# A hybrid decoder layer on one core: the work on the memory tiles tied behind the weight splits of the output products, and six of eight squares of x emitted behind the next weights

## The chip, the cores and the metric

The kernel runs on one core of one Trainium2 chip. The metric is the device time of one execution in microseconds (us). The engines are PE (TensorE, the matrix multiplier, with its weight loads PEld), ACT (ScalarE), DVE (VectorE), POOL (GpSimd) and SP (SyncE, which here only issues DMAs). Each engine works through its own list of instructions in order, and waits where an instruction's semaphore has not come yet.

## The reference

A decoder layer on 512 tokens of width 1024, all in float32: a SwiGLU feed-forward block, a mixer with a state-space group and a differential-attention group side by side, a cross-attention into a fixed memory of 256 tokens, a second SwiGLU block and a final norm.

```
x = x + 0.5 * swiglu(rms_norm(x, norm_ffn1_w[l]), ffn1_w_in[l], ffn1_w_out[l])
x = x + hybrid_mixer(rms_norm(x, norm_mix_w[l]), w_in_mix[l], ...)
x = x + memory_cross_attention(rms_norm(x, norm_cross_w[l]),
                               rms_norm(mem, norm_mem_w[l]),
                               w_cq[l], w_ck[l], w_cv[l], w_co[l])
x = x + 0.5 * swiglu(rms_norm(x, norm_ffn2_w[l]), ffn2_w_in[l], ffn2_w_out[l])
return rms_norm(x, norm_final_w)
```

Two pieces of it matter here. `rms_norm(mem, norm_mem_w)` needs the sum of squares of the memory and the memory times its gain, and both depend on inputs alone, so they can be computed early. `rms_norm(x, norm_mix_w)` needs the sum of squares of x after the first feed-forward block.

## The kernel before, in words

**Products.** A float32 product is done as three products of reduced operands: every operand is split into a high part (`wh`, written by an ACT copy, line 155) and a low part (`wl`, the rest, written by a DVE subtraction, line 156), and PE adds high by high, high by low and low by high. So each weight tile of 128 x 1024 or 128 x 512 that a DMA brings (`wr`, six buffers) costs one ACT and one DVE instruction before PE can use it, and the high and low tiles have three buffers each.

**The first feed-forward block** is done in three thirds of its hidden width. Each third first makes hidden tiles (`ffn_quads`, products `qa`, `qe`, `qb`) and then multiplies them by the output weights (`out_blocks`, products `oa`, `oe`, `ob`). Both use a block scheme with seven products of sums in place of eight: `block_tiles` makes from a hidden tile the operands `g11`, `s31`, `s24` and `g` (a few DVE subtractions and four splits). In the last tile of a third these are made at once, between the last hidden product and the output products. `out_blocks` then runs seven products, in the program's names: `oa` with block 11 and `oe` with the operand S1 interleaved, `ob` with S2, `oa` with block 12, `ob` with S3, `oe` with S4, `ob` with block 22. Each product has its weights in two parts in the last third: one of 128 x 1024 (twelve matmuls of 512 columns) and one of 128 x 512 (six). After a product, `update` adds its result to a tile of x on DVE, and on the last third calls `each`, which is `square`: an ACT square of that x tile with a running sum (`junk`, `squares`), for the mixer's norm.

**Work beside it.** When the last third reaches its output products, two generators are spawned. `prepare` builds a table of position biases, which ends with a DMA from DRAM to DRAM of 2.6 MB on ACT's queue (`rel_z`, line 609). `memory_in` loads the memory (four DMAs) and then, for each of eight memory tiles, emits under `behind(recent)` a square (ACT, `nacc` for the first tile and `nsq` for the others), the addition of the square to a sum (DVE, `nacc`) and a split of the tile times its gain (`hm`, ACT line 159 and DVE line 160). After the feed-forward block PE transposes x back (`pxf`) and multiplies the memory keys (`pck`, eight products, each with a weight tile `in_wck`).

**What sets the order.** `Order` runs the generator of matmuls and the spawned ones by a hand-kept clock. That is the order in which instructions are recorded; a scheduler may then put the instructions of ACT, DVE and PE in another order, while SP and POOL keep the recorded one. `behind(ins)` ties what is recorded in its block behind the instructions `ins` on the same engine. `recent` is a list that holds the two split instructions of the newest weights from `load_w`; the weights of `out_blocks` come from its own function `weights`, which leaves `recent` as it is.

Of the kernel before, what the change touches and what calls it, by code (L numbers as in the profile page):

```python
# [100 lines left out]
def body(tc, a, dbg=None):  # L101
# [13 lines left out]
    def nm(s):  # L115
        uid[0] += 1
        return f"{s}_{uid[0]}"

    def s2(s, dt=F32, shape=(P, T)):
        if math.prod(shape[1:]) <= T // 2:  # L120
            return sp.tile(list(shape), dt, tag="s1", name=nm(s), bufs=NHALF)
        return sp.tile(list(shape), dt, tag="s2", name=nm(s))
# [17 lines left out]
    last, start, last_sum, recent, newest, newest_mm = [], [], [], [], [], []  # L140
    V, S, G = nc.vector, nc.scalar, nc.gpsimd
    od = Order()
# [9 lines left out]
    def split_into(hi, lo, src, scale=None):  # L152
        if scale is None:
            return (
                S.activation(hi, src, AF.Copy),  # L155
                V.tensor_tensor(lo, src, hi.bitcast(F32), ALU.subtract),  # L156
            )
        return (
            S.activation(hi, src, AF.Copy, scale=scale),
            V.scalar_tensor_tensor(lo, src, scale, hi.bitcast(F32), ALU.mult, ALU.subtract),  # L160
        )
# [388 lines left out]
    squares = small("squares", 8, bufs=1)  # L550

    def square(tb, n):
        junk = s2("junk")
        S.activation(junk, x[4 * n + tb], AF.Square, accum_out=squares[:, 4 * n + tb : 4 * n + tb + 1])

    def fin1():
        od.spawn(normed(st_mix, C_MIX, h, squares), 2.0)
        od.spawn(block_sums_in_dram(), 10.0)

    od.spawn(st1.finish(), 18.0)  # L560
    od.add(ffn1(h1, wa_s, beside, square, fin1))


# [641 lines left out]
    def out_blocks(blocks, sums, g, col4, ncol4, each=None, finale=None, clean=True):  # L1205


        n = len(g)
        parts = [(k, min(k + 2, n)) for k in range(0, n, 2)]

        def fetch(of, part):
            raw = wp.tile([P, (part[1] - part[0]) * T], F32, tag="wr", name=nm("wr"), bufs=6)
            nc.sync.dma_start(raw, of[:, part[0] * T : part[1] * T])
            return raw

        def weights(of, part, raw=None):
            if raw is None:
                raw = of(part) if callable(of) else fetch(of, part)
            w = raw.shape[1]
            hi = wp.tile([P, w], R32, tag="wh", name=nm("wh"))  # L1220
            lo = wp.tile([P, w], R32, tag="wl", name=nm("wl"))
            split_into(hi, lo, raw)
            return hi, lo

        def some(ps, w, which, part, t, first):
# [9 lines left out]
        def product(ps, of, which, first=False):  # L1235
            for part in parts:
                w = weights(of, part)
                for t in range(2):
                    yield from some(ps[t], w, which, part, t, first)
# [74 lines left out]
        with tc.manual_schedule(engines={mybir.EngineType.DVE, mybir.EngineType.Activation}):  # L1314
            yield from at_last(parts, blocks, sums, e_ps, b_ps, fetch, weights, some, update, finale)
# [156 lines left out]
```

## Time and profile before

| | |
|---|---|
| median of 3 runs | 1328.78 us (1328.25 to 1331.37) |
| the profiled execution, its time | 1328.03 us |
| its span, first to last instruction | 1326.2 us |
| mean granted clock of PE | 0.992 |
| busy in the span: PE, DVE, ACT, POOL | 98%, 75%, 53%, 10% |

Times in the trace count from the span's start. A row of a timeline gives the start, the duration, the engine, the line, the operation, output <- input, and in brackets how long the engine sat idle before it and what ended that wait. Rows that follow one another and are alike are merged, with their count and total. The granted clock is 1.00 when PE gets its full clock. Matmuls overlap: the distance between two starts is what one costs, not its own duration.

The output products of the last third of the first feed-forward block begin at 312.65 us in this trace, and the memory keys at 362.47 us.

### The profile page before, as it was taken

To read this page: it belongs to the slowest core of one execution; us is meant where nothing else is said; L and a number is where in the kernel's file an instruction comes from. 1 tells how busy PE (TensorE), PEld (TensorE's weight loads), DVE (VectorE), ACT (ScalarE), POOL (GpSimd) and SP (SyncE) were. 2 spreads that over 40 slices of the span, in tenths; PEclk is the share of its full clock that TensorE was granted. 3 is DMA by queue.
4 is the path that set the end of the run, shared out by engine and by line. 5 is a ranking of instruction groups with operands and counts; after the bars stand their busy time and mean duration, and the time that the engine had idled before them with its cause. 6 is when DMAs were issued, how large, how long until landed. Compare 5 with 4: busy or idle time off the path is not lost.

```text
span 1326.2 us, 20148 instructions
## 1 busy us (share of the span) xinstructions
PE 1296.8 (98%) x7728; PEld 1128.5 (85%) x7728; DVE 988.7 (75%) x1570; ACT 708.6 (53%) x1192; POOL 127.5 (10%) x143
## 2 busy tenths in 40 slices
PE   9999999997999999999999999999999999999996
PEld 7898998896797778777788877888889999989995
DVE  6988789787786586557867787645678878877886
ACT  6544556455654475346644556434465645555564
POOL 0001000000030011010112121120001000000001
PEclk9999999998999999999999999999999999999998
DMA  7557767874794523763465547784238876666662
GB/s 272 159 172 212 178 174 204 216 202 112 238 325 152 170 64 96 250 179 96 96 190 183 166 136 222 206 203 147 65 96 242 227 234 176 190 194 178 187 204 86
DMA packets 69432, 235.29 MB, mean 177 GB/s; under 512 B 8072, under 2 KB 9576, under 8 KB 68984
## 3 DMA queue, kind: packets, MB, share of 16 engines
q1 hardware_dynamic: 52912, 180.19, 40.4%
q0 software_dynamic: 12880, 44.62, 18.9%
q10 hardware_dynamic: 3544, 9.20, 2.0%
q8 instruction: 61, 1.00, 0.3%
q14 instruction: 35, 0.29, 0.1%
HBM read 231.82 MB, written 50.91 MB: 213 GB/s over the span
## 4 chain that ended last, share of the span: by engine, by line
PE 88%; issue 6%; DVE 3%; ACT 1%; POOL 1%; DMA 0%; POOLq 0%; SPq 0%; ACTq 0%; DVEq 0%
PE qb L240 12%; PE pm L146 9%; PE qe L240 8%; PE qa L240 8%; PE ob L1232 6%; PE pxbc L146 5%; PE oe L1232 4%; PE oa L1232 4%; PE pk L146 3%; PE pq L146 3%; PE pcq L146 3%; PE pv L146 3%; PE pz L146 2%; PE pck L146 2%; PE pa L146 2%
## 5 line engine op out<-in xcount | busy, mean ns | idle before, releaser
L155 ACT ACTIVATE wh<-wr 128x1024 fp32r<-128x1024 f32 (+1 forms) x329 | 334.7, 1020 | 367.5 <-issue 55.8
L156 DVE TENSOR_TENSOR wl<-wr,wh 128x1024 fp32r<-128x1024 f32 (+1 forms) x329 | 386.0, 1176 | 143.0 <-ACT wh L155 138.1
L146 PE MATMUL pxbc<-hnh,wh 128*128 128x512 f32 x128 | 52.3, 408 | 0.0
L146 PE MATMUL pxbc<-hnh,wl 128*128 128x512 f32 x128 | 50.3, 393 | 0.0
L146 PE MATMUL pxbc<-hnl,wh 128*128 128x512 f32 x128 | 50.2, 392 | 0.0
L741 ACT ACTIVATE ec<-ec,mn 128x512 f32<-128x512 f32 (+3 forms) x64 | 35.4, 555 | 24.1 <-DVE mn L740 24.0
L240 PE MATMUL qe<-s31h,wl 128*128 128x256 f32 x152 | 43.1, 283 | 0.0
L240 PE MATMUL qa<-h11h,wh 128*128 128x256 f32 x152 | 43.1, 283 | 0.0
L240 PE MATMUL qa<-hmh,wh 128*128 128x256 f32 x152 | 43.0, 283 | 0.0
L240 PE MATMUL qa<-hml,wh 128*128 128x256 f32 x152 | 43.0, 283 | 0.0
L240 PE MATMUL qa<-hmh,wl 128*128 128x256 f32 x152 | 43.0, 283 | 0.0
L240 PE MATMUL qb<-s31l,wh 128*128 128x256 f32 x152 | 43.0, 283 | 0.0
L240 PE MATMUL qb<-s31h,wl 128*128 128x256 f32 x152 | 43.0, 283 | 0.0
L240 PE MATMUL qe<-s24h,wh 128*128 128x256 f32 x152 | 43.0, 283 | 0.0
L240 PE MATMUL qe<-s24l,wh 128*128 128x256 f32 x152 | 43.0, 283 | 0.0
L240 PE MATMUL qe<-s24h,wl 128*128 128x256 f32 x152 | 43.0, 283 | 0.0
L240 PE MATMUL qb<-hmh,wh 128*128 128x256 f32 x152 | 43.0, 283 | 0.0
L240 PE MATMUL qb<-hml,wh 128*128 128x256 f32 x152 | 43.0, 283 | 0.0
L240 PE MATMUL qb<-hmh,wl 128*128 128x256 f32 x152 | 43.0, 283 | 0.0
L240 PE MATMUL qa<-h11h,wl 128*128 128x256 f32 x152 | 43.0, 283 | 0.0
L240 PE MATMUL qb<-s31h,wh 128*128 128x256 f32 x152 | 43.0, 283 | 0.0
L240 PE MATMUL qa<-h11l,wh 128*128 128x256 f32 x152 | 43.0, 283 | 0.0
(447 smaller groups left out, 4188.6 us busy)
## 6 DMA issues: line engine op xcount, KB each, us to landing
wr<-in_f2q SPq DMA_DIRECT2D x44, 512.0 KB, 4.3
wr<-in_f1q SPq DMA_DIRECT2D x40, 512.0 KB, 4.5
wr<-in_f1b SPq DMA_DIRECT2D x30, 512.0 KB, 4.6
isum<-in_f2q SPq DMA_DIRECT2D x22, 512.0 KB, 6.0
wr<-isum SPq DMA_DIRECT2D x22, 512.0 KB, 6.4
wsum<-in_f2b SPq DMA_DIRECT2D x20, 512.0 KB, 5.9
wr<-wsum SPq DMA_DIRECT2D x20, 512.0 KB, 4.6
wr<-in_f1q POOLq DMA_DIRECT2D x16, 512.0 KB, 7.0
```

The costliest lines, as they stand in the source:

```text
L146: newest_mm[:] = [nc.tensor.matmul(out, w, x, start=start, stop=stop).ins]
L155: S.activation(hi, src, AF.Copy),
L156: V.tensor_tensor(lo, src, hi.bitcast(F32), ALU.subtract),
L240: newest_mm[:] = [nc.tensor.matmul(out, a_[:, wc], b_, start=first and f == 0 and kp == 0 and j == 0, stop=kp == n - 1 and j == 2, skip_gr ...
L741: S.activation(ec[:, :n], ec[:, :n], AF.Exp, bias=mn, scale=-1.0, accum_out=sm[c][:, i : i + 1])
L1232: newest_mm[:] = [nc.tensor.matmul(ps, a_[:, ts], b_[:, ws], start=first and k == 0 and j == 0, stop=k == n - 1 and j == 2, skip_group_che ...
```

## The change

```diff
@@ square
     def square(tb, n):
+        if n == 0 and tb > 1:
+            list(square_of(tb, n))
+        else:
+            od.spawn(square_of(tb, n), 2.0)
+
+    def square_of(tb, n):
         junk = s2("junk")
         S.activation(junk, x[4 * n + tb], AF.Square, accum_out=squares[:, 4 * n + tb : 4 * n + tb + 1])
+        yield 0.0
@@ weights, in out_blocks
             hi = wp.tile([P, w], R32, tag="wh", name=nm("wh"))
             lo = wp.tile([P, w], R32, tag="wl", name=nm("wl"))
-            split_into(hi, lo, raw)
+            recent[:] = [i.ins for i in split_into(hi, lo, raw)]
             return hi, lo
```

The first edit records the square of an x tile 2.0 us of the hand-kept clock after its update, for six of the eight tiles; the last two (x2 and x3) are squared at once as before. The second makes `recent` hold the split of the newest output weights, so that each memory tile's square, sum and split are tied behind it. No instruction is added or removed on any engine. The instructions that stand in another order all lie between the last hidden tile of the first feed-forward block and the memory keys.

First place: ACT, at the start of the last third's output products. `wh_596` is the high part of the weights of `oe` (the first product that PE has to wait for there), `wh_599`, `wh_602`, `wh_605` belong to the parts that follow; `nacc`, `nsq` and `hm` are the memory tiles' squares and split. Before:

```order
L155 ACTIVATE gh_576_3407<-th_567_3384 128x512
L382 ACTIVATE nacc_608_3521<-mem2_591_3438 128x256
L159 ACTIVATE hm_609_3523<-mem2_591_3438,par_77 128x256
L385 ACTIVATE nsq_618_3559<-mem2_591_3438 128x256
L385 ACTIVATE nsq_623_3585<-mem2_592_3440 128x256
L385 ACTIVATE nsq_630_3618<-mem2_592_3440 128x256
L385 ACTIVATE nsq_640_3656<-mem2_593_3442 128x256
L385 ACTIVATE nsq_645_3680<-mem2_593_3442 128x256
L385 ACTIVATE nsq_651_3708<-mem2_594_3444 128x256
L385 ACTIVATE nsq_661_3754<-mem2_594_3444 128x256
L155 ACTIVATE wh_596_3455<-wr_595_3452 128x1024
L155 ACTIVATE wh_599_3473<-wr_598_3471 128x512
```

And with the change:

```order
L155 ACTIVATE gh_576_3407<-th_567_3384 128x512
L155 ACTIVATE wh_596_3455<-wr_595_3452 128x1024
L155 ACTIVATE wh_599_3473<-wr_598_3471 128x512
L155 ACTIVATE wh_602_3486<-wr_601_3483 128x512
L155 ACTIVATE wh_605_3503<-wr_595_3452 128x1024
L1296 ACTIVATE ob_582_3415<-oa_578_3411 128x512
L382 ACTIVATE nacc_608_3521<-mem2_591_3438 128x256
L1296 ACTIVATE ob_583_3416<-oa_579_3412 128x512
L159 ACTIVATE hm_609_3523<-mem2_591_3438,par_77 128x256
L155 ACTIVATE wh_611_3534<-wr_601_3483 128x512
```

The nine memory instructions that stood between the last operand split `gh` and the first weight split have moved behind the weight splits, and are spread one by one over the rest of the products. On DVE it is the same: one `hm` and seven `nacc` stood between `gl` and `wl_597`, and now none does.

Second place: ACT, ahead of the product `oe` with S4, whose first weights are `wh_638` before and `wh_636` now. `x0`, `x1` are updated after block 12, `x6`, `x7` after S3, the product right ahead of S4. Before:

```order
L155 ACTIVATE wh_633_3630<-wr_632_3627 128x512
L609 DMA rel_z_240<-rel_d_239 1024x1x640
L554 ACTIVATE junk_625_3597,squares_56_235<-x0_79 128x512
L554 ACTIVATE junk_626_3600,squares_56_235<-x1_83 128x512
L159 ACTIVATE hm_631_3621<-mem2_592_3440,par_77 128x256
L554 ACTIVATE junk_635_3642,squares_56_235<-x6_103 128x512
L554 ACTIVATE junk_636_3645,squares_56_235<-x7_107 128x512
L155 ACTIVATE wh_638_3649<-wr_637_3647 128x1024
```

And with the change:

```order
L155 ACTIVATE wh_633_3630<-wr_632_3627 128x512
L616 DMA rel_z_240<-rel_d_239 1024x1x640
L560 ACTIVATE junk_630_3623,squares_56_235<-x0_79 128x512
L560 ACTIVATE junk_631_3625,squares_56_235<-x1_83 128x512
L155 ACTIVATE wh_636_3645<-wr_635_3643 128x1024
L385 ACTIVATE nsq_638_3652<-mem2_593_3442 128x256
L159 ACTIVATE hm_639_3655<-mem2_593_3442,par_77 128x256
L560 ACTIVATE junk_640_3667,squares_56_235<-x6_103 128x512
```

The squares of x6 and x7 have moved from ahead of the S4 weights to behind them.

Third place: DVE, over the products with S3 and into S4. `wl_629` and `wl_634` before, `wl_627` and `wl_634` now, are the low parts of S3's weights; `wl_639` before and `wl_637` now is that of S4's first part. Before:

```order
L160 SCALAR_TENSOR_TENSOR hm_624_3588<-mem2_592_3440,par_77,hm_624_3588 128x256
L156 TENSOR_TENSOR wl_629_3606<-wr_627_3602,wh_628_3605 128x1024
L1243 SCALAR_TENSOR_TENSOR x0_79<-oa_578_3411,col4_73_412,x0_79 128x512
L1243 SCALAR_TENSOR_TENSOR x1_83<-oa_579_3412,col4_73_412,x1_83 128x512
L156 TENSOR_TENSOR wl_634_3631<-wr_632_3627,wh_633_3630 128x512
L1243 SCALAR_TENSOR_TENSOR x6_103<-ob_582_3415,ncol4_74_413,x6_103 128x512
L1243 SCALAR_TENSOR_TENSOR x7_107<-ob_583_3416,ncol4_74_413,x7_107 128x512
L160 SCALAR_TENSOR_TENSOR hm_631_3621<-mem2_592_3440,par_77,hm_631_3621 128x256
L156 TENSOR_TENSOR wl_639_3650<-wr_637_3647,wh_638_3649 128x1024
```

And with the change:

```order
L386 TENSOR_TENSOR nacc_608_3521<-nacc_608_3521,nsq_623_3585 128x256
L160 SCALAR_TENSOR_TENSOR hm_624_3588<-mem2_592_3440,par_77,hm_624_3588 128x256
L156 TENSOR_TENSOR wl_627_3602<-wr_625_3598,wh_626_3601 128x1024
L1250 SCALAR_TENSOR_TENSOR x0_79<-oa_578_3411,col4_73_412,x0_79 128x512
L1250 SCALAR_TENSOR_TENSOR x1_83<-oa_579_3412,col4_73_412,x1_83 128x512
L386 TENSOR_TENSOR nacc_608_3521<-nacc_608_3521,nsq_628_3614 128x256
L160 SCALAR_TENSOR_TENSOR hm_629_3617<-mem2_592_3440,par_77,hm_629_3617 128x256
L156 TENSOR_TENSOR wl_634_3631<-wr_632_3627,wh_633_3630 128x512
L1250 SCALAR_TENSOR_TENSOR x6_103<-ob_582_3415,ncol4_74_413,x6_103 128x512
L1250 SCALAR_TENSOR_TENSOR x7_107<-ob_583_3416,ncol4_74_413,x7_107 128x512
L156 TENSOR_TENSOR wl_637_3646<-wr_635_3643,wh_636_3645 128x1024
```

One sum `nacc` now stands ahead of `wl_627`, a sum and a split stand ahead of `wl_634`, and no memory instruction stands between the update of x7 and the low part of S4's weights. On PE a single pair of matmuls has changed places: in the second part of S3 the third matmul of `ob_582` now comes after the first of `ob_583`.

## The prediction

> **What bounds the kernel now.** I read the page first, then PE's waits over the whole span, then the timelines where the two longest of them lie.
>
> ```profile
> span 1326.2 us, 20148 instructions
> PE 1296.8 (98%) x7728; PEld 1128.5 (85%) x7728; DVE 988.7 (75%) x1570; ACT 708.6 (53%) x1192; POOL 127.5 (10%) x143
> PE oe L1232 <- ACT wh L155: 9.8, 2, 7.3
> ...
> PE oe L1232 <- DVE wl L156: 1.4, 2, 0.9
> ```
>
> PE is busy 1296.8 of 1326.2 us. The two lower rows, from the view of waits (total, times, longest), say that 9.8 + 1.4 = 11.2 us of the 29.4 us in which PE idles fall on two products `oe`. Both are in the stretch that the change reorders. The first is the interleaved start of the output products:
>
> ```profile
> 314.94 0.39 PE L1232 MATMUL oa<-wh,g11l 128*128 128x512 f32 x1
> 315.17 0.39 PE L1232 MATMUL oa<-wl,g11h 128*128 128x512 f32 x1
> 322.84 0.80 PE L1232 MATMUL oe<-wh,s31h 128*128 128x512 f32 x1 [7.29 <-ACT wh L155]
> ...
> 324.92 0.80 PE L1232 MATMUL oe<-wl,s31h 128*128 128x512 f32 x1 [0.86 <-DVE wl L156]
> 325.52 0.63 PE L1232 MATMUL oe<-wh,s31h 128*128 128x512 f32 x1
> 325.94 0.63 PE L1232 MATMUL oe<-wh,s31l 128*128 128x512 f32 x1
> ```
>
> PE stops at 315.56, restarts at 322.84 when the first high part is there, and runs on from 324.92 when the low part is. After the gap matmuls start 0.42 us apart (325.52 to 325.94), ahead of it 0.23 (314.94 to 315.17). The second gap is at the product with S4:
>
> ```profile
> 345.13 0.39 PE L1232 MATMUL ob<-wl,s31h 128*128 128x512 f32 x1
> 348.07 0.50 PE L1232 MATMUL oe<-wh,s24h 128*128 128x512 f32 x1 [2.54 <-ACT wh L155]
> ...
> 349.33 0.67 PE L1232 MATMUL oe<-wl,s24h 128*128 128x512 f32 x1 [0.53 <-DVE wl L156]
> ```
>
> The clock in slices (start:end, length, busy time of PE, PEld, DVE, ACT and POOL, then granted clock, DMA share, GB/s):
>
> ```profile
> 318.50:319.00 0.50, 0.00 (x0) 0.00 (x0) 0.49 (x1) 0.50 (x2) 0.00 (x0) 0.78 0.00 0
> 329.00:329.50 0.50, 0.50 (x4) 0.41 (x3) 0.00 (x0) 0.28 (x1) 0.00 (x0) 0.98 0.82 336
> 346.10:349.50 3.40, 0.91 (x3) 0.47 (x4) 2.06 (x4) 3.40 (x9) 0.00 (x0) 1.00 0.66 263
> 349.50:352.90 3.40, 3.40 (x9) 2.63 (x10) 2.30 (x4) 0.78 (x1) 0.00 (x0) 0.50 1.02 347
> 789.80:793.20 3.40, 2.31 (x11) 1.60 (x10) 3.40 (x5) 1.33 (x2) 2.04 (x3) 1.00 0.02 6
> ```
>
> A mean of 0.78 between 1.00 and 0.50 puts the first drop at 318.78, and 0.98 puts the return at 329.01. The second dip lasts from 349.50 to 352.90. So each gap costs twice: the idle time, and then matmuls at half clock.
>
> **The first gap.** What stands ahead of the first weight split on ACT and DVE:
>
> ```profile
> 318.90 0.40 ACT L382 ACTIVATE nacc<-mem 128x256 f32<-128x256 f32 x1
> ...
> 319.61 2.24 ACT L385 ACTIVATE nsq<-mem 128x256 f32<-128x256 f32 x7
> 321.75 2.08 ACT L155 ACTIVATE wh<-wr 128x1024 fp32r<-128x1024 f32 x3
> 320.14 3.59 DVE L386 TENSOR_TENSOR nacc<-nacc,nsq 128x256 f32<-128x256 f32 x7
> 323.65 1.22 DVE L156 TENSOR_TENSOR wl<-wr,wh 128x1024 fp32r<-128x1024 f32 x1
> ```
>
> The nine memory instructions hold ACT from 318.90 to 321.75. They are gone from there, so the split starts at 318.90, and PE follows it by what it does now, 322.84 - 321.75 = 1.09 us: 319.99. DVE has only an `hm` between its last operand split and 320.14, so the low part starts when the high part is done, at about 320.00 in place of 323.65. PE follows by 324.92 - 323.65 = 1.27 us, at 321.27. **That is 324.92 - 321.27 = 3.65 us.** The raw weights were long there: no DMA moved a byte in the slice at 318.50. The idle time falls from 7.3 to 4.4 us, which with the clock's steps where they lie in this trace still drops it at 318.78; I leave the matmuls at half clock as many as they are.
>
> **What covers the moved work.** Nine ACT instructions of 0.3 to 0.4 us and eight DVE instructions of 0.4 to 0.5 us now lie among PE's matmuls from 325 on. Where the cover is thinnest, the S3 product:
>
> ```profile
> 338.21 0.91 ACT L159 ACTIVATE hm<-mem,par 128x256 fp32r<-128x256 f32 x2
> 339.01 1.06 ACT L155 ACTIVATE wh<-wr 128x1024 fp32r<-128x1024 f32 x1
> 340.10 1.23 DVE L156 TENSOR_TENSOR wl<-wr,wh 128x1024 fp32r<-128x1024 f32 x1
> 341.74 0.39 PE L1232 MATMUL ob<-wl,s31h 128*128 128x512 f32 x1
> ```
>
> The low part begins at 340.10 and could be used 1.27 later, at 341.37; PE uses it at 341.74, 0.37 to spare. The change puts one `nsq` (2.24 / 7 = 0.32) ahead of the high part, which leaves 0.05, and one `nacc` (3.59 / 7 = 0.51) on DVE beside it. Cost zero by this row; the upper bound is 0.51 - 0.37 = 0.14 if both fell on DVE's path. Without this cover every `nacc` would cost its 0.51 us.
>
> **The second gap.** Rows around it:
>
> ```profile
> 344.88 1.43 DVE L1243 SCALAR_TENSOR_TENSOR x<-ob,ncol,x 128x512 f32<-128x512 f32 x2 [1.64 <-PE ob L1232]
> 346.23 0.48 DVE L160 SCALAR_TENSOR_TENSOR hm<-mem,par,hm 128x256 fp32r<-128x256 f32 x1
> 348.05 1.22 DVE L156 TENSOR_TENSOR wl<-wr,wh 128x1024 fp32r<-128x1024 f32 x1 [1.34 <-ACT wh L155]
> 346.98 1.04 ACT L155 ACTIVATE wh<-wr 128x1024 fp32r<-128x1024 f32 x1
> ```
>
> Now ACT squares x6 and x7, which wait for DVE's updates at 344.88, and only then splits S4's weights at 346.98; the low part follows at 348.05. With the change the high part stands behind the squares of x0 and x1 alone and is there before PE asks. Late next is DVE: the low part stands right behind the updates of x6 and x7. PE's exchanged pair lets `ob_582` end one matmul later (0.23), so the updates start at 345.11 on the old clock and the low part at 345.11 + (346.23 - 344.88) = 346.46 in place of 348.05. **That is 1.59 us**, 5.24 in all. PE then idles about 1.7 us between the two high-part matmuls and the low part. When its raw weights land these rows do not tell, only that they are there at 346.98; the split starts where ACT's squares end, which is what holds it today, so I take zero. At worst they land just then, 346.98 - 3.65 on the new clock, and the 1.59 us of this gap are not won.
>
> **The clock at the second gap.** A stretch of 3.40 us with PE busy for 0.91 was followed by half clock, one with 2.31 by full clock. A gap of 1.7 us leaves any such stretch at least 1.7 us of work, and more where the gap falls over its end; that is nearer to 2.31 than to 0.91, so I take no drop. At stake is the half-clock stretch, 349.33 to 352.90, of which 1 - 0.23 / 0.42 is lost: **1.6 us**, with bounds 0 and 1.6.
>
> The Trainium skill ("TensorE: Matmul & The Clock Gate", section "What's actually happening") says that the clock is halved after at least one idle window of some 3.4 us, and that these windows run free of the program. By an idle window taken strictly, the drop at 349.50 should not have come, with 0.91 us of work in it: there the row decides. For the gap that is left both give no drop, and by the page the sum would be the same.
>
> **Behind the products.** The memory keys start earlier by the whole gain, and their weights must keep up:
>
> ```profile
> SPq L174 <- DMA rel_z<-rel_d: 13.4, 1, 13.4
> 339.96 0.74 ACTq L609 DMA_DIRECT2D rel_z<-rel_d  x1
> 366.18 0.81 SPq L174 DMA_DIRECT2D wr<-in_wck  x2
> wr<-in_wck SPq DMA_DIRECT2D x1, 512.0 KB, 4.6
> 378.26 8.64 PE pck L146 x72
> ```
>
> SP stands for 13.4 us until the bias table's DMA has landed, 26.2 us after its issue, and only then asks for the weights of the sixth key product, which PE starts at 378.26 (3 of 8 products, 72 matmuls, are left). On ACT that DMA comes 3.65 us earlier less two `nsq` and one `hm` (0.32 + 0.32 + 0.46 at most) more ahead of it: 2.6 earlier, so SP is free at about 363.6. The weights land 4.6 us after their issue (the last column of that row), at 368.2, and take 1.0 for the high and 1.27 for the low part: 370.5. PE needs them at 378.26 - 6.8 = 371.5. Cost zero with 1.0 us to spare; if the DMA lands no earlier than now, 366.18 + 4.6 + 2.3 - 371.5 = 1.6 us of the gain are lost, the upper bound.
>
> The squares themselves are no matter: as many, on the same engine, with the last two recorded at once as before. Changes of order on SP and POOL: none.
>
> **The sum.** 3.65 + 1.59 + 1.6 = 6.8 us off the profiled execution: span 1326.2 to 1319.4, time 1328.03 to 1321.2. The median of the runs is 1328.78, 0.75 above this execution, so I forecast **1321.9 us**. What a measurement can tell from no change is about 0.3%, 4.0 us: faster means below 1324.8, slower above 1332.8.
>
> **Rivals.**
>
> *The clock drops at the second gap too.* Then 5.2 us are won, 1323.5. For it: half clock came after 0.91 us of work, and 1.7 lies in the unknown between. Against: 2.31 did not drop it. 0.17.
>
> *The clock does not drop at the first gap.* The changes at 318.78, 329.01 and 349.50 lie 3 and 6 times 3.41 us apart, a fixed grid; where it lies against the gap in another execution I cannot know. A gap of 4.4 us holds a whole step wholly idle in (4.4 - 3.41) / 3.41, 30%, of the positions, and one with up to 0.91 us of work in 56%. So no drop has at most 0.44, and less as the limit lies above 0.91. It saves 1 - 0.23 / 0.42 of the time from 324.92 to 329.01, 1.9 us more: 8.7 in all, 1320.1. The page named above says that one idle window is needed, which would make this rival likelier. 0.14.
>
> *Weights come late.* S4's raw weights (1.6), the sixth key product (1.6) or S3 (0.14) take part of it back: one or two of these leave 3.6 to 5.2 us, around 1324.4. For it: 1.0 us and 0.05 us of room. 0.10.
>
> *The wait moves on.* The memory work falls on the path among the products: seven `nacc` at 0.51 give 3.6 us back, and the S4 weights are late as well: no more than the 1.6 of the clock is won, 1327 to 1329, no change. Against: PE runs without a stop from 324.92 to 345.5, and the low part that is nearest to being late has 0.37 us of room. 0.10.
>
> *Slower.* The spread memory tiles each stand ahead of a split that PE wants at once, ACT's `nsq` and DVE's `nacc` one after the other: 7 x (0.32 + 0.51) = 5.8 us, in pieces that leave PE too little work for full clock in two more stretches, 3.2 us. Less the 3.65 of the first gap that is 5.4 us slower, 1334.2. It decides from the point where a tile costs more than the 0.37 us of room at every split, which at 0.32 on ACT and 0.51 on DVE, in parallel, they hardly do. 0.07.
>
> **How the numbers follow.** The forecast has 0.42. Faster by over 0.3%: 0.42 + 0.17 + 0.14 and half of the late weights, 0.78; the same 0.15; slower 0.07. The range is 1319.0 to 1326.5: the lower end takes in the first gap at full clock with an execution 1 us under the median, the upper one the late weights with both prices; what is left out is the wait that moves on and the slower case, some 0.17.
>
> **What would show it.** In the new trace: the first ACT split of `wr` right behind `gh` near 318.9, `oe` from 320.0 and steadily from 321.3; an idle stretch of some 1.7 us in `oe` with S4, ended by DVE `wl` and not by ACT `wh`; the granted clock 1.00 in and behind that stretch; PE without a wait over 16 us between the two gaps; the memory keys starting 6.8 us earlier than 362.47, and no wait of PE before the sixth key product. PE's waits on `oe` should sum to about 6.2 us in place of 11.2 (4.4 before the first high part, next to nothing before its low part, 1.7 at S4). I am wrong if a new wait of PE on `wl` or `wh` stands between 325 and 342, if SP's wait for `rel_z` holds the key products, or if what is won there is lost again later in the span.

## The result and the profile after

| | before | with the change |
|---|---|---|
| median of 20 runs each | 1329.62 us (1327.90 to 1332.67) | 1327.99 us (1323.30 to 1331.08) |
| ratio, 95% interval | | 0.9982, 0.9973 to 0.9992 |
| profiled execution: time, span | 1328.03, 1326.2 us | 1326.33, 1324.2 us |

The change wins 1.6 us by the medians and 2.0 us by the spans, a small gain whose interval lies clear of no change. 6.8 us were forecast; the time lies outside the predicted range. First the page of the changed kernel:

```profile
span 1324.2 us, 20141 instructions
PE 1295.8 (98%) x7728; PEld 1127.3 (85%) x7728; DVE 988.1 (75%) x1570; ACT 708.4 (53%) x1192; POOL 124.8 (9%) x143
```

Its view of PE's waits (total, times, longest):

```profile
PE oe L1239 <- ACT wh L155: 4.4, 1, 4.4
PE pck L146 <- DVE wl L156: 3.8, 1, 3.8
...
PE oe L1239 <- DVE wl L156: 1.7, 1, 1.7
```

On `oe` PE now waits 4.4 + 1.7 = 6.1 us in place of 11.2, but a wait of 3.8 us in the key products `pck` is new. The first gap, in the timeline:

```profile
318.12 0.61 ACT L155 ACTIVATE gh<-th 128x512 fp32r<-128x512 f32 x1
318.64 2.08 ACT L155 ACTIVATE wh<-wr 128x1024 fp32r<-128x1024 f32 x3
...
319.73 0.80 PE L1239 MATMUL oe<-wh,s31h 128*128 128x512 f32 x1 [4.44 <-ACT wh L155]
320.32 0.63 PE L1239 MATMUL oe<-wh,s31l 128*128 128x512 f32 x1
320.99 0.80 PE L1239 MATMUL oe<-wl,s31h 128*128 128x512 f32 x1
...
342.91 0.50 PE L1239 MATMUL oe<-wl,s24h 128*128 128x512 f32 x1 [1.73 <-DVE wl L156]
```

The weight split stands right behind `gh`, `oe` follows 1.09 us after it, and the matmul with the low part follows without a gap. The last row is the second gap, 1.73 us, ended by `wl` and no longer by `wh`. The clock, in slices (granted clock third from the end):

```profile
319.50:320.00 0.50, 0.27 (x1) 0.27 (x2) 0.33 (x2) 0.50 (x2) 0.00 (x0) 0.65 0.00 0
323.00:323.50 0.50, 0.50 (x4) 0.41 (x3) 0.50 (x2) 0.00 (x0) 0.00 (x0) 0.94 0.74 283
...
341.00:344.40 3.40, 1.67 (x8) 1.23 (x7) 3.40 (x7) 3.30 (x8) 0.00 (x0) 1.00 0.87 285
343.00:346.40 3.40, 3.40 (x15) 2.83 (x16) 3.40 (x8) 3.22 (x7) 0.00 (x0) 1.00 0.78 292
```

By 0.65 and 0.94 the clock was at half from 319.65 to 323.06, one step of 3.41 us; before it was three (318.78 to 329.01). At the second gap it stayed at 1.00. So the keys come earlier, by more than forecast, and then PE stops (timeline of the change):

```profile
354.42 0.50 PE L146 MATMUL pck<-hm,wh 128*128 128x256 f32 x2
...
370.35 0.50 PE L146 MATMUL pck<-hm,wh 128*128 128x256 f32 x2 [0.15 <-ACT wh L155]
374.65 0.58 PE L146 MATMUL pck<-hm,wl 128*128 128x256 f32 x1 [3.80 <-DVE wl L156]
...
384.46 0.40 PE L146 MATMUL pq<-hnh,wh 128*128 128x512 f32 x1
```

And the end of the same stage in the kernel before, where `pq` is the first product of the mixer:

```profile
386.73 0.40 PE L146 MATMUL pq<-hnh,wh 128*128 128x512 f32 x1
```

The keys start at 354.42 against 362.47, 8.05 us earlier. The next stage starts at 384.46 against 386.73, 2.27 us earlier. **From `pck` to `pq` it takes 30.04 us where it took 24.26: 5.78 us are lost there.** PE idles for 3.95 of them (0.15 + 3.80), and most of the rest goes by half clock behind the stop (0.51 over 374.20 to 377.60). From `pq` to the end both traces take the same within 0.3 us. What PE waited for, in the chain of waits of the change from 361.51 on:

```profile
361.51 7.64 DMA wr<-in_wck
...
369.23 1.06 ACT wh L155
370.29 0.53 ACT hnh L155
...
370.85 0.56 DVE hnl L156
...
371.45 0.74 DVE hf L415
372.20 0.60 DVE hnl L156
372.80 0.13 DVE hf L415
...
373.38 1.23 DVE wl L156
...
374.65 1.43 PE pck L146 x5
```

The weights of the sixth key product are issued at 361.51, land 7.64 us later, are split by ACT, and then their low part stands on DVE behind two `hnl` and two `hf` (the mixer's normed x). Who issues what just then, in the change:

```profile
335.08 0.74 ACTq L616 DMA_DIRECT2D rel_z<-rel_d  x1
...
358.97 1.62 POOL L357 TENSOR_TENSOR ncol<-nv,mhalf 128x2 f32<-128x2 f32 x1 [3.18 <-DVE nv L355]
360.56 0.92 POOL L1209 DMA_DIRECT2D isum<-in_f2q  x1
361.51 0.81 SPq L174 DMA_DIRECT2D wr<-in_wck  x2
```

What SP waited for ahead of that last row, in the view of its waits:

```profile
SPq L174 <- DMA rel_z<-rel_d: 14.5, 1, 14.5
```

And POOL's row of the same kind in the kernel before, where SP issued the sixth weights at 366.18:

```profile
367.04 1.62 POOL L357 TENSOR_TENSOR ncol<-nv,mhalf 128x2 f32<-128x2 f32 x1 [3.19 <-DVE nv L355]
368.62 0.93 POOL L1202 DMA_DIRECT2D isum<-in_f2q  x1
```

`isum` on POOL's queue is a 512 KB addition for the block sums of the second feed-forward block's weights. In the kernel before it was issued 2.44 us behind the sixth weights, now 0.95 us ahead of them. It stands on POOL behind `ncol`, which belongs to the key stage (the addition follows the first `pck` by 6.14 us now and 6.15 before), so it moved with the keys; SP's weights moved with `rel_z`, which ends SP's wait and came only 4.88 us earlier.

### The profile page after: what moved, and what is told of

The parts are those of the page before. It is cut to its first block, busy times and chain, and to the rows that moved or that the text cites. A ratio compares the mean times of both kernels' runs of the same rounds, so it can differ in the third digit from the quotient of the medians.

```text
span 1324.2 us, 20141 instructions
## 1 busy us (share of the span) xinstructions
PE 1295.8 (98%) x7728; PEld 1127.3 (85%) x7728; DVE 988.1 (75%) x1570; ACT 708.4 (53%) x1192; POOL 124.8 (9%) x143
## 4 chain that ended last, share of the span: by engine, by line
PE 86%; issue 7%; DVE 4%; DMA 1%; ACT 1%; POOL 1%; POOLq 0%; ACTq 0%; DVEq 0%
PE qb L240 12%; PE pm L146 9%; PE qe L240 8%; PE qa L240 8%; PE ob L1239 6%; PE pxbc L146 5%; PE oe L1239 4%; PE oa L1239 4%; PE pk L146 3%; PE pq L146 3%; PE pcq L146 3%; PE pv L146 3%; PE pz L146 2%; PE pa L146 2%; PE pg L146 2%
## 5 line engine op out<-in xcount | busy, mean ns | idle before, releaser
L240 PE MATMUL qb<-s24h,wl 128*128 128x256 f32 x152 | 43.0, 283 | 0.0
L240 PE MATMUL qb<-s24l,wh 128*128 128x256 f32 x152 | 43.0, 283 | 0.0
L240 PE MATMUL qb<-s24h,wh 128*128 128x256 f32 x152 | 43.0, 283 | 0.0
```

What stands on the lines that cost most here:

```text
L240: newest_mm[:] = [nc.tensor.matmul(out, a_[:, wc], b_, start=first and f == 0 and kp == 0 and j == 0, stop=kp == n - 1 and j == 2, skip_gr ...
```

## The experiments

In the table, "POOL" is the issue of that addition less the issue of the sixth key weights, and `pck` to `pq` the length of the key stage, each from the one profiled execution. The ratio is to the kernel before on the same chip.

| kernel | median us | ratio, 95% interval | POOL us | `pck` to `pq` us |
|---|---|---|---|---|
| before | | | +2.44 | 24.26 |
| the change | 1327.99 | 0.9982 (0.9973 to 0.9992) | -0.95 | 30.04 |
| squares alone | 1330.11 | 0.9995 (0.9982 to 1.0007) | -0.80 | 32.28 |
| memory alone | 1325.57 | 0.9962 (0.9948 to 0.9975) | +1.92 | 24.27 |
| before, isum later | 1330.78 | 1.0011 (1.0002 to 1.0020) | moved | 24.27 |
| memory alone, isum later | 1325.27 | 0.9974 (0.9963 to 0.9984) | moved | 24.25 |
| squares alone, isum later | 1325.90 | 0.9978 (0.9969 to 0.9987) | moved | 24.25 |
| the change, isum later | 1322.75 | 0.9951 (0.9938 to 0.9964) | moved | 24.26 |
| before, POOL's sums later | 1328.95 | 1.0001 (0.9992 to 1.0009) | moved | 24.26 |
| the change, POOL's sums later | 1322.93 | 0.9951 (0.9938 to 0.9964) | moved | 25.33 |

**The bias table on another queue.** The first idea was that SP's wait for `rel_z` alone is at fault, and that another queue would free SP: in the change and, as control, in the kernel before.

```diff
-        S.dma_start(rel_z[:, :, :RW], ...
+        G.dma_start(rel_z[:, :, :RW], ...
```

> The changed kernel with one edit: the DMA that writes the bias table (rel_z) is issued by POOL instead of ACT, so that no DMA of SP shares its semaphore. Theory A (the gain of about 8 us at the start of the memory keys is real and is taken back because SP holds the sixth key product's weights until rel_z has landed): SP asks for these weights near 350 us, PE's wait of 3.8 us in pck and the half clock behind it go, the queries start 7 to 8 us earlier than in the kernel before, and the time is 6 to 8 us under the kernel before, near 1322. Rival B (the weights are late because the DMA engines are busy with other transfers there, whatever SP waits for): the wait in pck stays at 2 us or more and the time stays within 3 us of the kernel before. Rival C (executions scatter with the place of the clock's steps, and the gaps' gain was never 8 us): no wait in pck, and still within 4 us of the kernel before.

> The kernel before with the same edit alone, as a control. Theory A: in the kernel before the sixth product's weights were asked for late but came in time, so the time stays within 1.5 us of the kernel before. Rival B: the same. If the edit itself made the kernel faster (less traffic in ACT's queue), this run would be 4 us or more faster and e1 would tell nothing of the wait.

Measured: 1352.68 us, ratio 1.0164 (1.0148 to 1.0180), and the control 1356.99 us, 1.0195 (1.0181 to 1.0209). The control became slower by itself: with `rel_z` on POOL's queue PE waits for weights in many key products, also in the kernel before (its waits):

```profile
PE pck L146 <- ACT wh L155: 4.1, 4, 1.0
...
PE pck L146 <- DVE wl L156: 3.0, 4, 0.8
```

The pair says nothing of SP's wait.

**Each half of the change alone.** Squares alone, with the second edit undone:

```diff
-            recent[:] = [i.ins for i in split_into(hi, lo, raw)]
+            split_into(hi, lo, raw)
```

and memory alone, with `square` as it was before.

> The first edit alone: the squares behind the next weights, the memory tiles as before. Theory A: the first gap stays at 7.3 + 0.9 us, the second falls from 3.1 to about 1.7 us, the clock does not drop there, and the memory keys start 3 to 3.5 us earlier against the operand splits; rel_z is issued no earlier than before, so the sixth key product waits for its weights, up to 2 us, and the time is 1 to 3.5 us under the kernel before. Rival C: within 1 us of the kernel before.

> The second edit alone: the memory tiles tied behind the output weights, the squares as before. Theory A: the first gap falls to 4.4 us, 3.65 won; the second gap stays near 3 us, and the clock drops there or not by the place of its steps; the keys start 3 to 5 us earlier, rel_z about 3 us earlier, so the sixth key product waits 0 to 2 us, and the time is 2 to 4 us under the kernel before. Rival C: within 1 us.

The squares alone gain nothing that can be told from zero, where 1 to 3.5 us were forecast. Their trace starts the keys at 358.03, 4.44 us earlier than before, and loses it in the key stage (waits of PE):

```profile
PE pck L146 <- DVE wl L156: 3.8, 1, 3.8
...
PE pck L146 <- ACT wh L155: 1.0, 1, 1.0
```

One of the twelve executions of the squares alone took 4846.7 us, and why is not known; the median in the table leaves it out (with it 1330.57). The memory edit alone gains 5.1 us, where 2 to 4 were forecast, more than both edits together, with no wait in `pck`. So the loss is no fixed cost of an edit; it appears where the keys come early and `rel_z` does not come early with them: with the squares alone the keys start 4.44 us earlier and `rel_z` is issued 0.69 earlier, with the memory alone it is 4.76 and 4.49. In both kernels that lose, POOL's addition is ahead of the sixth weights; in both that do not, it is behind them.

**The block sums later.** SP waits for `rel_z` at the sixth weights because the program's DMAs share a few semaphores in turn, and two block-sum copies (`isum` on SP) among the key weights bring the turn of `rel_z`'s to that DMA. SP's list in the change, with the semaphores waited for (`wr_725` holds the sixth weights, and `rel_z`'s DMA counts up `DMAHW1_49`):

```
L1205 DMA isum00_246<-in_f2q 16x8192 [waits DMAHW5_49]
L174 DMA wr_703_3932<-in_wck 128x1024 [waits DMAHW6_49,DMAHW0_49,DVE_49]
L174 DMA wr_713_3975<-in_wck 128x1024 [waits DVE_49]
L1205 DMA isum10_248<-in_f2q 16x8192
L174 DMA wr_725_4025<-in_wck 128x1024 [waits DMAHW1_49,DVE_49]
```

With the block sums later it is `wr_725_4023<-in_wck 128x1024 [waits DVE_49]`, and the eighth weights stand behind `rel_z` instead. The edit:

```diff
-        od.spawn(block_sums_in_dram(), 10.0)
+        od.spawn(block_sums_in_dram(), 30.0)
```

> The change, with the DMAs that build the sums of the second block's weights (isum) recorded later, behind the key weights. By this the weights of the sixth key product no longer stand eight DMAs behind the bias table's DMA (rel_z), so SP doesn't wait for it there; rel_z itself stays where it is, on ACT's queue, with the same bytes. Theory A (the queue): what the change won is lost because SP stands 14.5 us on rel_z. Then the sixth key product starts without a wait of PE over 0.5 us, pck starts near 354.4 as in the change, the clock does not drop near 375, pq starts near 379 in place of 384.6, and the time is 5 to 6 us under the change: 1322 to 1323.5. Theory B (the traffic): the 2.6 MB of rel_z fill the DMA engines, and the sixth weights land near 369 whoever issues them. Then a wait of PE of 3 us or more stays before the sixth product, and the time stays near 1328. Theory C (what is won early is lost later whatever happens): no wait before the sixth product, and still less than 2 us won, 1326 to 1328, with another wait in its place.

> The kernel before, with the same move of the isum DMAs: what that edit is worth by itself. Theory A: nothing, since PE did not wait in the key products there: 1329.6, within 1.5 us, keys from 362.5 and pq near 386.9. Theory B: the same. If it is over 2 us faster or slower, the run with the change has to be read against this one and not against the kernel before.

> The memory tiles' work behind the weight splits alone (squares as before), with the same move of the isum DMAs. Theory A: this half of the change had no wait left in the key products, so there is nothing more to win: 1325.6, within 1 us of that half without the move. The two edits together with the move must then be faster than this by what the second gap gives, 1.6 us without and 3.2 us with its clock: it is the squares' worth when nothing takes it back. Theory B: the same time, but the two edits together no faster than this.

> The six squares behind the next weights alone (the memory tiles as before), with the isum DMAs recorded later, so that the sixth key weights don't stand behind rel_z on SP. Theory A (the queue): this half lost what it won, 4.4 us at the start of the keys, in a wait before the sixth key product. With that wait gone, pck to pq takes 24.3 us, as in the kernel before, in place of 32.4, and the time is 3 to 4.5 us under the kernel before: about 1326. Theory C (the squares' gain is lost later whatever happens): the time stays within 1 us of the kernel before.

The stall is gone in the change, which falls to 1322.75 us, and in the squares alone, which now gain. The edit itself costs 0.1% in the kernel before. Against that control the halves are worth 0.37% (1.0011 - 0.9974) and 0.33% (1.0011 - 0.9978), and both together 0.60%: nearly their sum (the squares ran on another chip than the control, each against the kernel before on its own), where without the move they were worth 0.38%, 0.05% and 0.18%. Theory C, that the gain is lost later whatever happens, fell. But the edit took away SP's wait and POOL's addition at once; which of them made the stall stayed open.

**POOL's additions later, SP's wait kept.** The block sums keep a lead of `LEAD` copies on SP ahead of the additions on POOL. With eight in place of four, SP's list is the same through the key weights, POOL's two small loads that follow the addition (2 and 16 KB) stay, and only the addition is gone from there:

```diff
-LEAD = 4
+LEAD = 8
```

> The change, with a lead of eight in place of four between the block-sum copies on SP and the additions to them on POOL's queue. SP's list is the same up to the key weights, so SP still waits for rel_z before the sixth key weights; POOL's first addition of 512 KB no longer starts 0.95 us before them. Theory A (SP's wait alone): SP is free near 361.5 in a trace with the keys from 354.4, the stall before the sixth product stays (2 us or more) and the time is near that of the change, 1328. Theory D (both together: SP's wait makes the weights late and POOL's transfer, which overtakes them, makes them later): the weights land 4.6 us after their issue and not 7.6, near 366.1, before the high part is asked for at 370; no wait of PE over 0.5 us before the sixth product, pck to pq 24.3 us, and the time is 5 us under the change, about 1322.5. In between (a stall near 1 us): both count by themselves.

> The kernel before, with the same lead of eight. In it POOL's addition came 2.4 us behind the sixth key weights and PE did not wait there, so by both theories the time stays within 2 us of 1329.6. What it differs by is the price of the later additions themselves, in the rest of the program.

Rows of the change with the later additions, first its waits of SP and of PE, then its timeline (the last row is in the sixth product):

```profile
SPq L174 <- DMA rel_z<-rel_d: 14.1, 1, 14.1
...
PE pck L146 <- DVE wl L156: 0.6, 2, 0.3
```

```profile
364.95 0.81 SPq L174 DMA_DIRECT2D wr<-in_wck  x2
...
369.01 1.06 ACT L155 ACTIVATE wh<-wr 128x1024 fp32r<-128x1024 f32 x1 [2.51 <-DMA wr<-in_wck]
...
374.43 0.38 PE L146 MATMUL pck<-hm,wl 128*128 128x256 f32 x1 [0.34 <-DVE wl L156]
```

SP still waits 14.1 us for `rel_z`, and issues the sixth weights 6.87 us after the first `pck` (358.08), about as late as in the change (7.09). Yet ACT's split, which waits for them, starts 4.06 us after their issue and not 7.72, and PE waits 0.34 us at the sixth product and not 3.8; with a wait of 0.23 us at the eighth this is all. The time is that with the block sums later, and the control does not move. **That is mainly theory D: SP's wait makes the weights late, which costs 25.33 - 24.26 = 1.1 us in the key stage, and POOL's addition ahead of them makes it 5.8.** No run keeps the addition there and takes SP's wait away, so what the addition costs by itself is not shown.

**Filling the first gap.** To see what the clock's drop there is worth, PE multiplies a tile of ones during the wait; the results are overwritten. The block sums are later in all four. Part of the edit, with twelve:

```diff
+                if each is not None and part is parts[0] and m is both[0]:
+                    with behind(list(newest_mm)):
+                        for _ in range(12):
+                            nc.tensor.matmul(b_ps[1], ones_r, ...
```

> The change with the isum DMAs later, and twelve matmuls of a tile of ones, 128 x 512, into a PSUM tile that is overwritten later, behind the first six pairs of oa: PE works 2.8 us of the 4.4 us in which it waits for the first weights of oe. They add to the work and change no result. If the clock falls there because a stretch of 3.4 us was all but idle, it stays at 1.00 now, the matmuls from 321 to 325 start 0.23 us apart in place of 0.42, and the time is 1.9 us under that without the filling, about 1320.5. If the drop has another cause, the clock still falls and the time is the same within 0.5 us. If the extra matmuls are in the way, oe starts later than 320 and the time is above by as much.

> As with the twelve matmuls of ones, with eighteen of them: PE works 4.1 us of the 4.4 in the first gap. With twelve the clock still fell, behind a step of 3.4 us with 1.21 us of work in it. If the limit lies between 1.21 and 2.31 us of work per step, the clock stays at 1.00 now (at most 1.7 us of idle time are left), the matmuls behind the first low part start 0.23 us apart, and the time is 1.6 us under that with the isum DMAs later alone, about 1321. If it falls all the same, what drops it is not the share of work, and the time is the same within 0.5 us.

Measured: 1322.82 us (ratio 0.9953, 0.9942 to 0.9965) with twelve and 1325.33 us (0.9975, 0.9965 to 0.9984) with eighteen, no gain. The condition on `each` holds in the second feed-forward block too, and there the same matmuls stand where there is no gap (timeline with eighteen):

```profile
1273.22 4.30 PE L1295 MATMUL ob<-ones_r 128*128 128x512 f32 x18
```

With `and finale is None` they stand in the first block alone:

> The change with the isum DMAs later and the twelve matmuls of ones, now in the first feed-forward block alone. In the two runs before, the same matmuls also stood in the last third of the second block, where PE has no gap to hide them: twelve cost 2.8 us there, eighteen 4.1 us, and the traces show them at 1272 us. If that alone kept the filling from paying, the time is 2.8 us under that run, 1320.0, and 2 to 3 us under the version without a filling (1322.75). If the filling itself gains nothing, the time is 1322.5 or more.

> The same with eighteen matmuls, in the first block alone. By the copy in the second block the run before was 4.1 us too long, which leaves 1321.2. If the clock's drop is worth what its rows say (1.6 us for a step of 3.4 us), this is 1 to 2 us under the one with twelve, where one step at half clock was left. If the two are equal within 1 us, the placement of the clock's steps in an execution decides more than the filling.

Measured: 1321.03 us (0.9941, 0.9924 to 0.9958) and 1320.12 us (0.9931, 0.9920 to 0.9943), 1.8 and 5.2 us less than with the copy in the second block, whose matmuls take some 2.8 and 4.1 us there. The two lie 0.9 us apart, too close to tell one from the other. Windows of PE with twelve (first two rows; the clock falls at about 321.3) and, in the fence behind, with eighteen:

```profile
317.90:321.30 3.40, 1.34 (x5) 0.48 (x3) 3.13 (x6) 3.14 (x5) 0.00 (x0) 1.00 0.00 0
321.30:324.70 3.40, 3.27 (x8) 2.59 (x9) 3.02 (x5) 0.00 (x0) 0.00 (x0) 0.51 0.26 77
```

```profile
316.20:319.60 3.40, 3.08 (x15) 2.21 (x13) 3.06 (x7) 2.87 (x5) 0.00 (x0) 1.00 0.00 0
319.60:323.00 3.40, 2.87 (x12) 2.06 (x13) 3.40 (x5) 0.90 (x2) 0.00 (x0) 1.00 0.17 33
323.00:326.40 3.40, 3.40 (x17) 2.81 (x16) 2.77 (x5) 3.21 (x6) 0.00 (x0) 1.00 0.74 248
```

With eighteen the clock does not fall in this trace. That version has the lowest time of all, 9.5 us under the kernel before on its chip, and beats the change; against the block sums later without a filling (0.9951) the intervals still overlap, so what the filling adds, 1 to 3 us, is not settled.

## Why the prediction went wrong, step by step

- **First gap, 3.65 us: right.** The forecast wait of 4.4 us was 4.44, and the low part follows at 320.99 where 321.27 was forecast, in a trace that runs 0.26 us earlier up to there (314.68 against 314.94 for the same `oa`).
- **The cover: right.** PE works through from 321 to 341 (10.00 us of each 10.00):

```profile
321.00:331.00 10.00, 10.00 (x39) 7.44 (x40) 8.42 (x12) 5.20 (x10) 1.74 (x2) 0.90 0.50 130
331.00:341.00 10.00, 10.00 (x45) 7.95 (x43) 8.80 (x16) 7.92 (x17) 0.00 (x0) 1.00 0.81 235
```

- **Second gap, 1.59 us, and its clock, 1.6 us: right, the clock by little.** 1.73 us of idle time for 1.7 forecast, ended by `wl`, and the clock at 1.00 behind it. The matmul that ends the gap starts 6.42 us earlier (349.33 to 342.91) and the keys 8.05, so the clock is worth 1.63. The step with the gap in it holds 1.68 us of work; in another run three steps with 1.62 to 1.63 were followed by half clock (last section).
- **The first gap's clock: mis-sized.** I left the half-clock matmuls as many as they were. In this execution one step of 3.41 us was at half clock and not three. Behind the first low part, half clock now lasts 2.07 us (320.99 to 323.06) and not 4.09 (324.92 to 329.01): (4.09 - 2.07) x (1 - 0.23 / 0.42) = 0.9 us more. With it and the 0.26 us by which this trace runs earlier ahead of the gap, the keys should start 6.8 + 0.9 + 0.3 = 8.0 us earlier; they start 8.05 earlier. The 0.9 us are luck of where the steps lay: with the block sums later the same gap of 4.4 us was followed by two steps, and half clock lasts 5.3 us behind the first low part (323.36 to 328.63). Rows of both steps:

```profile
321.90:325.30 3.40, 3.16 (x7) 2.05 (x8) 3.23 (x5) 1.19 (x3) 0.00 (x0) 0.50 0.14 20
325.30:328.70 3.40, 3.40 (x10) 2.63 (x9) 0.94 (x2) 1.05 (x1) 0.00 (x0) 0.51 0.71 235
```

- **"Behind the products", cost zero with 1.0 us to spare, at most 1.6: this is the step that failed.** It cost 5.78 us. Three terms of it were wrong. The weights were to "land 4.6 us after their issue"; they took 7.64. The split was to take 1.0 and 1.27 us; from landing to PE it took 374.65 - 369.15 = 5.5, because the splits of `hnh` on ACT and four instructions on DVE stand ahead of the low part. And the stop brought half clock with it, which had no term. SP itself was free at 361.51, earlier than the 363.6 forecast: its wait was not underrated. The length of the split could be read in the trace of before (rows of the sixth product there):

```profile
372.18 1.06 ACT L155 ACTIVATE wh<-wr 128x1024 fp32r<-128x1024 f32 x1 [1.28 <-PE pck L146]
...
376.41 1.22 DVE L156 TENSOR_TENSOR wl<-wr,wh 128x1024 fp32r<-128x1024 f32 x1
...
378.33 0.28 PE L146 MATMUL pck<-hm,wl 128*128 128x256 f32 x1
```

From the start of the high part to the end of the low part that is 376.41 + 1.22 - 372.18 = 5.45 us, and PE uses the low part 0.7 us later. With 5.45 in place of 2.27 the prediction's own sum gives 368.2 + 5.45 = 373.7 against 371.5: 2.1 us lost, and not 1.0 to spare.

- **What I overlooked** stands in one sentence of the prediction: "Changes of order on SP and POOL: none." Within each queue that is so. Between them the order turned round: POOL's addition is tied to the key stage and moved 8.05 us earlier, SP's weights are tied to `rel_z` and moved 4.67 (366.18 to 361.51). The margin of 2.44 us in the trace of before was there to be read, and I read no row of POOL.
- **The rivals.** "Weights come late" named the place, at 0.10 and 1.6 us; its price was too low by 4.2 us. The rest of the sum stands, to about 1 us: with POOL's additions or the block sums out of the way the change runs at 1322.93 and 1322.75 us, where 1321.9 was forecast.

That the addition ahead of the weights delays them, when SP issues them late, is shown by its removal; by which way, no run shows. The landing was 7.64 us with it 0.95 us ahead, 4.6 with it 2.44 us behind, and ACT's split started 4.06 us after the issue without it. The Trainium skill ("DMA: Bandwidth & Descriptors", section "SWDGE vs HWDGE vs iDMA") says that POOL's queue and SP's feed different queues inside each DMA engine, and that the engine takes them in turn. By that a transfer already under way shares the engines with the weights, which agrees with 7.64 against 4.6.

## What to carry to other kernels

A stage that moves earlier takes along all that is tied to it, on the queues of SP and POOL too, and leaves what is tied to something else: compare, for each transfer that the later stage needs, how far it and its neighbours on other queues move, and look for pairs whose order turns round. A transfer's margin ends where the consumer has its operand, so the in-order work that stands ahead of the split on ACT and DVE belongs in it, and a stop can cost about half as much again in clock (here 3.95 us idle and 1.8 more). When two halves of a change gain less together than one alone, look for two transfers whose order the new timing turns round.

## What the runs showed of the hardware

The clock of PE fell behind steps of 3.41 us with 0.91 us of work in them (before) and with 1.34 (twelve matmuls of ones). It did not fall behind one with 1.68: in the change the steps counted on from 319.65 put one at 340.13 to 343.54, and the gap of 1.73 us from 341.18 to 342.91 lies wholly in it. In the kernel before with the bias table on POOL's queue, three steps with 1.62, 1.62 and 1.63 us of work (from 376.37, 383.20 and 390.02) were each followed by half clock. By these traces the limit lies between 1.63 and 1.68 us, near half of the step; PE's busy time is itself modelled in a profile, so the second decimal is not certain. The Trainium skill ("TensorE: Matmul & The Clock Gate", section "What's actually happening") speaks of an idle window; by these rows it need not be idle.

The same DMA of 2.6 MB, from DRAM to DRAM, costs 24 to 26 us of the whole kernel when it is issued from POOL's queue rather than from ACT's (1.0164 - 0.9982 = 1.82% in the change, 1.95% in the kernel before); why, no run here shows.
